# Modulation vectors moved from VectorE to TensorE, in a diffusion trunk on one Trainium2 core

## The chip, the cores and the metric

The kernel runs on one core of a Trainium2 chip. The metric is the device time of one execution in microseconds (us), taken as the median of several runs. A profile of one execution of the kernel before stands beside the runs.

## What is computed

The reference is one step of a trunk of two layers, over 512 latent tokens and 128 context tokens of 1024 features. A layer is a feed-forward half, a token mixer and a second feed-forward half. Each of the three is modulated by the condition and is followed by a layer norm:

```
def _modulation(cond, w, b):
    return (jax.nn.silu(cond) @ w + b).reshape(cond.shape[0], N_MOD, D_MODEL)

def _modulate(x, shift, scale):
    return x * (1.0 + scale[:, None, :]) + shift[:, None, :]

def _ffn_half(x, mod, slot, w1, w3, w2, g, b):
    h = _modulate(x, mod[:, 3 * slot], mod[:, 3 * slot + 1])
    f = (jax.nn.silu(h @ w1) * (h @ w3)) @ w2
    return _residual_post_norm(x, f, mod[:, 3 * slot + 2], FFN_RES, g, b)
```

There are nine modulation vectors a layer (shift, scale and gate for each of the three), for two conditions, one of the latent tokens and one of the context. `w_mod` is 1024 by 9 x 1024 for each layer, 75 MB in all. The mixer has three groups of heads: A (differential attention), B (windowed, with a sink) and C (keys and values from a compressed tensor).

## The kernel before, in words

**Layout.** Features lie on partitions in eight tiles `x[d]` of 128 by 640 tokens. Every product with a weight is done in three passes (weight hi by input hi, hi by lo, lo by hi), so each weight tile is cast on ScalarE (`wh`, L299) and the remainder taken on VectorE or GpSimd (`wl`, L306). One stream (`Stream`, L220) loads the tiles on SP's queue into two raw buffers, in the order of their products, and converts up to six blocks ahead.

**A feed-forward half** (`ffn`, L1016) goes through 22 hidden tiles in six chunks (`CHUNKS`). The first three tiles are done in the plain way; each of the other 19 is a `Pair` (L830): seven products of twelve matmuls of 320 columns, in Winograd's scheme, with the sums `pm`, `sl` and `gf` that VectorE forms from the banks (`op`, L858). `start` (L893) issues a pair's first two products, `run` (L898) the other five. What waits for a product is put in `later` and issued by `slot` (L815) after the next product. After each chunk `rows` (L631) or, in the last, `rows_norm` (L659) multiply by w2 and add to `x`. L1110 scales the gate after the first chunk, and L527 is the first product of the next norm's statistics. There are four halves, F1 to F4 in the order of the program, and a mixer after F1 and after F3.

**A modulation unit** is one vector for one feature tile, written (layer, vector, tile): 128 values for each of two conditions. There are 144. It is made in one of three ways.

1. `mod_start` (L406): sixteen passes on TensorE (`mod_mm`, L391, L397), of eight float32 matmuls with 32 weight columns each, put 128 values on four rows of a bank. VectorE copies them to `ms`. `mod_finish` (L380) puts them on partitions with a matmul with `sel` (L384) into a new bank, and VectorE adds the bias (L389). The start of the program and the first chunk of F1 use this, for 24 units.
2. `mod_beside` (L411): the same in the unused part of a bank that holds the fifth transpose of an attention unit (`Unit.t5`, L1578, and in group B where a unit has three blocks of keys). The passes go to TensorE at once; `rest` (L419), issued later, is on ScalarE: the bias for the last unit and the copy of this one. `mix_left` says how many may be started.
3. `vec_mods` (L437): VectorE multiplies rows of the transposed weights (`wmt`) by the condition that was put on all partitions (`condb`) and sums them, four instructions of 512 columns a unit (L460) and a last one (L463). `mods` (L1025), which the half calls between products, takes its next steps.

Of the 144 units, 24 go the first way, ten the second (all in mixer 0) and 110 the third: 38 in F1, 36 in F2 and 36 in F3. F4 has none.

**Loads.** `mod_load(k)` (L365) issues two loads of 256 KB for each of the next k units that aren't loaded, on SP's queue, into a pool `pm` of four buffers, two units. `mod_mm` calls it before its matmuls and after them, with the depth `mod_depth[0]`, 2. In the same queue stand the weights, the copies between partitions that the attention needs, and the transfers of `x`.

**The order in a mixer** is written out in `SCHEDULES`, one table for each layer: a letter and a number issue a stage of a unit of attention (`s` scores, `t` four transposes, `r` the fifth one with `mod_beside`, `R` its `rest`, `p` values). 40 of the 48 units of a mixer call `mod_beside`: 16 of group A, 8 of B, 16 of C.

Of the kernel before, what the change touches and what calls it, by code (L numbers as in the profile page):

```python
# [7 lines left out]
F32 = mybir.dt.float32  # L8
# [97 lines left out]
def trunk_kernel(tc, I, O):  # L106
# [3 lines left out]
    with ExitStack() as es:  # L110
# [98 lines left out]
        class W:  # L209
            """a weight tile in pieces along its contraction tiles"""  # L210
# [9 lines left out]
        class Stream:  # L220
            """jobs in the order of their products: whole tiles, or the blocks a pair of tiles is combined to"""
# [28 lines left out]
            def combine(self, r):  # L250
                """the sums of Winograd's scheme of two tiles' halves along the contraction"""
# [85 lines left out]
        def step(n=1, fill=1):  # L337
            """the oldest task's next steps, as many of the filler, and a waiting transfer"""
            for _ in range(n):
                advance(tasks)  # L340
            for _ in range(fill):
                advance(filler)
            if dmaq:
                dmaq.pop(0)()

        def start(g):
            """a task whose first step comes at once"""
            next(g)
            tasks.append(g)
# [8 lines left out]
        modq = []  # L358
        mod_queue = [nc.sync]
        mod_depth = [2]  # L360
# [30 lines left out]
        def mod_mm(ps):  # L391
# [6 lines left out]
            mod_load(mod_depth[0])  # L398
# [7 lines left out]
        def mod_start():  # L406
            """128 modulation values of the next unit, before they are put on partitions"""
            ps = bank("mod")
            mod_take(mod_mm(ps[:, :P]), ps[:, :P])

        def mod_beside(ps):  # L411
            """the same in the unused part of a bank; gives what is left to do when the bank's products are issued"""
# [16 lines left out]
        def mod_step():  # L429
            """the rest of the last unit, and the start of the next"""  # L430
            mod_finish()
            if modq:
                mod_start()

        vecq = []

        def vec_mods(n):  # L437
            """generator: the next n units on the vector engine, beside the products of a feed-forward half"""
            cb = pv.tile([P, 4, NS], F32, tag="tabs", name=f"cb{uid()}")
            nc.sync.dma_start(out=cb, in_=I["condb"])  # L440
            yield
            units, w = [vecq.pop(0) for _ in range(n)], []

            def load(k):
                while len(w) < min(k, 2 * n):
                    t = pm.tile([P, 512], F32, tag="wm", name=f"wv{uid()}")
                    hf = len(w) % 2
                    nc.sync.dma_start(out=t, in_=I["wmt"][units[len(w) // 2]][:, 512 * hf:512 * hf + 512])
                    w.append(t)
            load(4)  # L450
            for i in range(4):
                S.activation(cb[:, i, :], cb[:, i, :], AF.Silu)
                yield
            scr = u(pq, f"scr{uid()}")[:, :512]
            for i, (l, s_, d) in enumerate(units):
                a = tiny([4], "va")
                for hf in range(2):
                    load(2 * i + hf + 4)
                    for st in range(2):
                        V.scalar_tensor_tensor(out=scr, in0=w[2 * i + hf], scalar=1.0, in1=cb[:, 2 * st + hf, :], op0=ALU.mult, op1=ALU.mult,  # L460
                                               accum_out=a[:, 2 * hf + st:2 * hf + st + 1])
                        yield
                V.scalar_tensor_tensor(out=mod[l][:, s_, d, :], in0=a[:, 0:2], scalar=bmod[:, l, s_, d:d + 1], in1=a[:, 2:4], op0=ALU.add,  # L463
                                       op1=ALU.add)

# [14 lines left out]
        def mmk(out, whl, acts, half, k, ka, n):  # L480
            """the three passes of contraction tile k (of n) into a half's bank"""
# [19 lines left out]
        def acc(d, half):  # L501
            """running sums of x and x^2 over feature tiles"""
# [27 lines left out]
        def bcast(name, src, nt):  # L530
            """[P, nt] per-token values (token on its partition) to every partition, along the tokens"""
# [34 lines left out]
        def mod_hi(d, half, h):  # L566
            """hi part of x * gamma + beta"""
# [5 lines left out]
        def mod_f(d, half, kept=None):  # L573
            """x * gamma + beta, in kept when it is to stay"""
# [56 lines left out]
        def rows(acts, n, begun, each):  # L631
            """x += gate * (w^T act) for every feature tile; begun: (weights, sums, contraction tiles done) of the first ones"""
# [17 lines left out]
        def open_tiles(pn, wn, h, half, d):  # L650
            """contraction tile d of the next phase's first weight tiles, the passes that need hi first"""
# [7 lines left out]
        def rows_norm(acts, n, l, ln, nxt, begun=()):  # L659
            """the same, then the layer norm; with nxt = (layer, slot), also the next modulated input and, tile by tile  # L660
            as it comes, the first weight tiles of the next phase; begun: (weights, sums, contraction tiles done) of the
            first feature tiles"""
# [62 lines left out]
            # first half: statistics under the second half's products  # L725
# [76 lines left out]
        def alpha_x(l, ln):  # L802
            """the residual branch of what the norm left in x"""
# [9 lines left out]
        later = []  # L813

        def slot():  # L815
            """what waited for the products issued so far"""
# [13 lines left out]
        class Pair:  # L830
            """silu(w1^T h) * (w3^T h) of one hidden tile by Winograd's scheme: rows w1, w3, columns the halves of the tokens"""
# [61 lines left out]
            def start(self):  # L893
                p1, p2 = bank("p1"), bank("p2")
                self.prod(p1, self.b11, lambda: S.copy(self.m[:, LO], p1[:, :HN]) and None)
# [30 lines left out]
            def run_first(self, mods, other, ts):  # L926
                """the same with the sums of the input's quarters last, as they come, and the start of the other one before them"""
# [43 lines left out]
        def tb_steps(tb, h):  # L971
            """generator: hi and lo of the sums of the input's quarters, for the contraction tiles k and k + 4; the last ones
            take the place of the quarter that no pair reads"""
# [42 lines left out]
        def ffn(l, f, h, first, nmod, nvec, norm, scale_x, tb, ts):  # L1016
            n_left = [nmod]
            vec, credit = [None], [0.0]
            if nvec:
                cb = vec_mods(nvec)  # L1020
                next(cb)
# [3 lines left out]
            def mods(when=None):  # L1025
                if vec[0]:
                    credit[0] += (4 * nvec + 4) / 95 * (1 if when is None else 1)
                    while credit[0] >= 1:
                        credit[0] -= 1
                        next(vec[0], None)  # L1030
# [15 lines left out]
            for ci, (j0, j1) in enumerate(CHUNKS):  # L1046
                gs = []
                n = j1 - j0
                for j in range(j0, j1):
                    if j >= NC:  # L1050
# [6 lines left out]
                        if j == NC:  # L1057
                            scale_x()
                            if nvec:
                                vec[0] = cb  # L1060
# [1140 lines left out]
```

## Time and profile before

| | us |
|---|---|
| three runs | 2775.0, 2775.86, 2776.04 |
| median | 2775.86 |
| span of the profiled execution | 2768.7 |
| TensorE busy | 2541.8 (92%) |
| VectorE busy | 2257.6 (82%) |
| GpSimd busy | 1249.4 (45%) |
| ScalarE busy | 1150.4 (42%) |

The span is the time from the first to the last instruction of one profiled execution; what lies around it in a run is not in it. An engine's busy time is the time in which it executes, with waits left out. A share over the whole span mixes the halves, the mixers and the norms, whose limits differ, so the rows below are cut by stage. In them PE is TensorE, PEld its weight loads, DVE VectorE, ACT ScalarE, POOL GpSimd and SP the engine that issues the transfers.

### The profile page before, as it was taken

The numbers are of one execution on the slowest core, as the hardware profiler recorded it, in microseconds if no ns is written. First come the engines' busy times: TensorE is split into PE (matmuls) and PEld (weight loads), VectorE is DVE, ScalarE is ACT, GpSimd is POOL, SyncE is SP. The second block draws the span as 40 slices with busy tenths as digits, with TensorE's granted clock in tenths as the row PEclk, the third lists the DMA queues.
The fourth block names the chain that finished last, engine by engine and source line by source line (L and its number), as shares of the span: only waits on it lengthen the run. The fifth ranks groups of instructions, "written<-read, shape, count | busy, mean of one in ns | idle before, by whom it ended". The sixth has DMA issues, their size and how long they took to land. (4 is left out here: it accounts for less than half of the span.)

```text
span 2768.7 us, 48136 instructions
## 1 busy us (share of the span) xinstructions
PE 2541.8 (92%) x17546; PEld 2430.0 (88%) x17546; DVE 2257.6 (82%) x4315; ACT 1150.4 (42%) x2474; POOL 1249.4 (45%) x973
## 2 busy tenths in 40 slices
PE   7998899899999998888999988998898899999997
PEld 6988899888868998888889888898897689999997
DVE  6699999865875889999988999999677758777776
ACT  5232323345575533333344333333455745344333
POOL 2343453521454644434545445434333556545545
PEclk9999999999999999999989999999999999999998
DMA  7333333334212133333323333333332121222222
GB/s 265 129 120 109 115 113 125 114 118 149 74 37 92 69 115 118 122 103 112 118 69 103 116 119 113 119 126 99 120 100 60 37 99 47 82 78 89 81 85 69
DMA packets 130539, 285.77 MB, mean 103 GB/s; under 512 B 16832, under 2 KB 34560, under 8 KB 129664
## 3 DMA queue, kind: packets, MB, share of 16 engines
q1 hardware_dynamic: 130304, 282.70, 31.3%
q8 instruction: 139, 2.28, 0.3%
q14 instruction: 96, 0.79, 0.1%
HBM read 254.95 MB, written 8.81 MB: 95 GB/s over the span
## 5 line engine op out<-in xcount | busy, mean ns | idle before, releaser
L306 DVE TENSOR_TENSOR wl<-wr,wh 128x512 fp32r<-128x512 f32 (+1 forms) x524 | 499.0, 965 | 66.3 <-ACT wh L299 64.5
L299 ACT CAST wh<-wr 128x512 fp32r<-128x512 f32 (+1 forms) x570 | 331.9, 606 | 500.8 <-DMA wr<-in_w 351.8
L485 PE MATMUL o<-gh,wh 128*128 128x256 f32 (+1 forms) x1408 | 442.8, 314 | 24.8 <-ACT gh L886 13.2
L847 PE MATMUL p<-hh,wh 128*128 128x320 f32 x1216 | 387.7, 319 | 83.3 <-DVE pm L858 79.1
L485 PE MATMUL o<-gl,wh 128*128 128x256 f32 (+1 forms) x1408 | 440.7, 313 | 3.2 <-DVE gl L478 1.8
L259 POOL TENSOR_TENSOR ws<-wr 128x512 f32<-128x512 f32 x76 | 111.3, 1464 | 728.4 <-DMA wr<-in_w 548.8
L485 PE MATMUL o<-gh,wl 128*128 128x256 f32 (+1 forms) x1408 | 438.1, 311 | 0.0
L460 DVE SCALAR_TENSOR_TENSOR scr<-wv,cb 128x512 f32<-128x512 f32 x440 | 394.7, 897 | 4.2
L847 PE MATMUL p<-hl,wh 128*128 128x320 f32 x1216 | 384.7, 316 | 6.6 <-DVE hl L1010 6.6
L847 PE MATMUL p<-hh,wl 128*128 128x320 f32 x1216 | 385.5, 317 | 1.9 <-DVE wl L306 1.8
L847 PEld LDWEIGHTS p<-hh,wh 128*128 128x128 f32 x1216 | 235.6, 194 | 92.3 <-issue 78.0
L306 POOL TENSOR_TENSOR wl<-ws,wh 128x512 fp32r<-128x512 f32 x152 | 241.4, 1595 | 133.3 <-ACT wh L299 133.3
L485 PEld LDWEIGHTS o<-gh,wh 128*128 128x128 f32 x1408 | 269.3, 191 | 33.6 <-ACT gh L886 16.0
L299 ACT CAST wh<-ws 128x512 fp32r<-128x512 f32 x304 | 181.3, 619 | 247.3 <-POOL ws L259 80.6
L485 PEld LDWEIGHTS o<-gl,wh 128*128 128x128 f32 x1408 | 269.5, 191 | 8.9 <-DVE gl L891 4.9
L485 PEld LDWEIGHTS o<-gh,wl 128*128 128x128 f32 x1408 | 269.1, 191 | 0.0
L610 DVE SCALAR_TENSOR_TENSOR x<-o,gat,x 128x128 f32<-128x128 f32 (+2 forms) x404 | 192.8, 523 | 92.9 <-PE o L485 87.4
L847 PEld LDWEIGHTS p<-hl,wh 128*128 128x128 f32 x1216 | 236.1, 194 | 7.6 <-DVE hl L1010 7.6
L847 PEld LDWEIGHTS p<-hh,wl 128*128 128x128 f32 x1216 | 235.9, 194 | 4.0 <-DVE wl L306 4.0
L877 ACT ACTIVATE sl<-sl 128x320 f32<-128x320 f32 x76 | 35.8, 471 | 277.7 <-DVE sl L858 277.5
L259 POOL TENSOR_TENSOR ws<-wr,ws 128x512 f32<-128x512 f32 x76 | 130.8, 1720 | 0.0
L306 DVE TENSOR_TENSOR wl<-ws,wh 128x512 fp32r<-128x512 f32 x152 | 129.3, 863 | 0.0
(428 smaller groups left out, 6618.8 us busy)
## 6 DMA issues: line engine op xcount, KB each, us to landing
wr<-in_w SPq DMA_DIRECT2D x176, 512.0 KB, 3.8
wv<-in_wmt SPq DMA_DIRECT2D x220, 256.0 KB, 2.8
wr<-in_w SPq DMA_DIRECT2D x128, 256.0 KB, 2.6
wm<-in_wmod SPq DMA_DIRECT2D x68, 256.0 KB, 5.0
wr<-in_w SPq DMA_DIRECT2D x64, 192.0 KB, 2.4
wr<-in_wint SPq DMA_DIRECT2D x24, 512.0 KB, 3.8
wr<-in_wo SPq DMA_DIRECT2D x16, 512.0 KB, 3.8
xd<-x SPq DMA_DIRECT2D x16, 320.0 KB, 5.6
```

The costliest lines, as they stand in the source:

```text
L259: G.tensor_tensor(out=o, in0=x0, in1=x1, op=op)
L299: S.copy(hl[0], src[:, c0:c1])
L306: eng.tensor_tensor(out=t2, in0=src, in1=t.bitcast(F32), op=ALU.subtract)
L460: V.scalar_tensor_tensor(out=scr, in0=w[2 * i + hf], scalar=1.0, in1=cb[:, 2 * st + hf, :], op0=ALU.mult, op1=ALU.mult, accum_out=a[:, 2 * ...
L485: PE.matmul(out[:, :cn], whl[a][:, k, :], b[:, c0:c0 + cn], start=k == 0 and i == 0, stop=k == n - 1 and i == 2)
L610: V.scalar_tensor_tensor(out=c, in0=src, scalar=gat[:, d, s:s + 1], in1=c, op0=ALU.mult, op1=ALU.add)
L847: PE.matmul(out[:, :HN], w[a][:, k, :], b[k][c], start=k == 0 and i == 0, stop=k == 3 and i == 2)
L877: S.activation(self.sl[:, HI], self.sl[:, HI], AF.Silu)
```

## The change

No unit is made on VectorE any more. 16 units go beside a pair's first product in each of F1, F2 and F3, with the second way's code: `Pair.start` calls `mod_beside` with the 192 columns of the bank that the product leaves free, ahead of the product, and `rest` follows the copy of the product. What is pending is finished by `mod_finish` in the middle of the pair. 40 units go beside the transposes of mixer 0 and 32 beside those of mixer 1. The lists are refilled before each half and each mixer (`next_mods`). After its matmuls `mod_mm` asks for one unit ahead and no longer two.

```
-        mod_depth = [2]
+        mod_depth = [2, 2]
...
             for kk in range(2):
                 for g in range(4):
                     PE.matmul(ps[32 * g:32 * g + 32, :], silc[:, 2 * g + kk, :], w[g // 2][:, 2 * (g % 2) + kk, :], start=kk == 0, stop=kk == 1)
-            mod_load(mod_depth[0])
+            mod_load(mod_depth[1])
...
-        def vec_mods(n):
...
-                        V.scalar_tensor_tensor(out=scr, in0=w[2 * i + hf], scalar=1.0, in1=cb[:, 2 * st + hf, :], op0=ALU.mult, op1=ALU.mult,
-                                               accum_out=a[:, 2 * hf + st:2 * hf + st + 1])
-                        yield
...
             def start(self):
                 p1, p2 = bank("p1"), bank("p2")
-                self.prod(p1, self.b11, lambda: S.copy(self.m[:, LO], p1[:, :HN]) and None)
+                rest = mod_beside(p1[:, HN:])
+
+                def c1():
+                    S.copy(self.m[:, LO], p1[:, :HN])
+                    rest()
+                self.prod(p1, self.b11, c1)
                 self.prod(p2, self.b21, lambda: self.c11(p2))
...
-        def ffn(l, f, h, first, nmod, nvec, norm, scale_x, tb, ts):
+        def ffn(l, f, h, first, nmod, nside, norm, scale_x, tb, ts):
             n_left = [nmod]
-            vec, credit = [None], [0.0]
-            if nvec:
-                cb = vec_mods(nvec)
-                next(cb)
+            mix_left[0] = nside
...
-                if vec[0]:
-                    credit[0] += (4 * nvec + 4) / 95 * (1 if when is None else 1)
-                    while credit[0] >= 1:
-                        credit[0] -= 1
-                        next(vec[0], None)
...
+        def next_mods(n):
+            modq.extend(later_mods.pop(0) for _ in range(n * KD))
+
         for l in range(DEPTH):
             if l:
+                next_mods(2)
                 tb, ts = tb_next
-            h, first = ffn(l, 0, h, first, *((8, 38) if l == 0 else (0, 36)), lambda a, n, b: rows_norm(a, n, l, 0, (l, 1), b),
+            h, first = ffn(l, 0, h, first, 0 if l else KD, 2 * KD, lambda a, n, b: rows_norm(a, n, l, 0, (l, 1), b),
                            alpha_first if l == 0 else lambda: alpha_x(l - 1, 2), tb, ts)
-            if l == 0:
-                modq += [vecq.pop(0) for _ in range(10)]
+            next_mods(4 if l else 5)
             h, first = mixer(l, h, first, lambda a, n, b: rows_norm(a, n, l, 1, (l, 2), b))
             nxt = (l + 1, 0) if l + 1 < DEPTH else None
+            if l == 0:
+                next_mods(2)
             tb, ts = tb_next
-            h, first = ffn(l, 1, h, first, 0, 36 if l == 0 else 0, lambda a, n, b: rows_norm(a, n, l, 2, nxt, b),
+            h, first = ffn(l, 1, h, first, 0, 0 if l else 2 * KD, lambda a, n, b: rows_norm(a, n, l, 2, nxt, b),
                            lambda: alpha_x(l, 1), tb, ts)
```

How the order of the instructions moves is seen at three places. The first is TensorE in F1, where one pair ends (its seventh product) and the next begins; `p` is a bank, `hh` and `hl` are the parts of the input, `wh` and `wl` those of the weights. Before:

```order
L847 MATMUL p_2706<-hh_196,wh_2589 128x320
L847 MATMUL p_2706<-hl_197,wh_2589 128x320
L847 MATMUL p_2706<-hh_196,wl_2590 128x320
L847 MATMUL p_2729<-hh_182,wh_2612 128x320
L847 MATMUL p_2729<-hl_183,wh_2612 128x320
```

And with the change, at such a place, and further on the end of the pair's fourth product and the start of its fifth:

```order
L818 MATMUL p_2517<-hh_196,wh_2410 128x320
L818 MATMUL p_2517<-hl_197,wh_2410 128x320
L818 MATMUL p_2517<-hh_196,wl_2411 128x320
L397 MATMUL p_2540<-wm_2381,silc 32x128 x2
L397 MATMUL p_2540<-wm_2383,silc 32x128 x2
L397 MATMUL p_2540<-wm_2381,silc 32x128 x2
L397 MATMUL p_2540<-wm_2383,silc 32x128 x2
L818 MATMUL p_2540<-hh_182,wh_2430 128x320
...
L818 MATMUL p_2611<-hh_184,wl_2500 128x320
L384 MATMUL mod_2630<-const,ms_2589 128x2
L818 MATMUL p_2633<-tvb_693,wh_2519 128x320
```

Eight matmuls of a unit now stand ahead of the pair's first product, and the one that puts its values on partitions stands between the fourth and the fifth.

The second place is VectorE in F1 beside a pair. `scr` is the result of a unit's multiplication that nothing reads, `wl` the low part of a weight block, the others are the pair's sums. Before:

```order
L858 TENSOR_TENSOR sl_1891<-pm_1830,p_1969 128x320
L306 TENSOR_TENSOR wl_1996<-ws_1938,wh_1995 128x512
L460 SCALAR_TENSOR_TENSOR scr_1514,va_1914<-wv_1806,cb_808 128x512 x2
L881 TENSOR_TENSOR gf_1966<-gf_1966,sl_1891 128x320
L858 TENSOR_TENSOR sl_2051<-pm_1989,p_1993 128x320
L306 TENSOR_TENSOR wl_2036<-wr_1946,wh_2035 128x384
L463 SCALAR_TENSOR_TENSOR mod_144<-va_1914,const 128x2
L460 SCALAR_TENSOR_TENSOR scr_1514,va_2075<-wv_1870,cb_808 128x512 x2
L306 TENSOR_TENSOR wl_2058<-wr_1948,wh_2057 128x384
```

And with the change:

```order
L829 TENSOR_TENSOR sl_2445<-pm_2376,p_2517 128x320
L306 TENSOR_TENSOR wl_2556<-ws_2487,wh_2555 128x512
L852 TENSOR_TENSOR gf_2515<-gf_2515,sl_2445 128x320
L829 TENSOR_TENSOR sl_2609<-pm_2537,p_2541 128x320
L306 TENSOR_TENSOR wl_2594<-wr_2495,wh_2593 128x512
L389 TENSOR_SCALAR mod_144<-mod_2630,const 128x2
L306 TENSOR_TENSOR wl_2614<-wr_2495,wh_2613 128x512
```

The multiplications are gone from between the pair's sums; what is left of a unit is one instruction of two columns.

The third place is SP's queue in mixer 0, where group C's queries and keys (`C1qh` to `C1kl`) are copied to their partitions. Before:

```order
L1890 DMA C1qh_9417<-qph_8614 32x512
L1891 DMA C1kh_9419<-kph_8479 32x640
L1890 DMA C1ql_9418<-qpl_8615 32x512
L1891 DMA C1kl_9420<-kpl_8480 32x640
L1256 DMA oh_9527<-oc_9529 64x2x128 x2
```

And with the change:

```order
L374 DMA wm_9558<-in_wmod 128x512
L374 DMA wm_9560<-in_wmod 128x512
L1854 DMA C1qh_9570<-qph_8636 32x512
L1855 DMA C1kh_9572<-kph_8475 32x640
L1854 DMA C1ql_9571<-qpl_8637 32x512
L1855 DMA C1kl_9573<-kpl_8476 32x640
L374 DMA wm_9636<-in_wmod 128x512
L374 DMA wm_9638<-in_wmod 128x512
L374 DMA wm_9694<-in_wmod 128x512
L374 DMA wm_9696<-in_wmod 128x512
L1220 DMA oh_9712<-oc_9714 64x2x128 x2
```

The loads of the units (`wm`) now stand ahead of and behind those copies in one queue.

## Rows read from the trace of the kernel before

**Rows 1.** The page's head: the span, then busy time, share, instructions.

```profile
span 2768.7 us, 48136 instructions
...
PE 2541.8 (92%) x17546; PEld 2430.0 (88%) x17546; DVE 2257.6 (82%) x4315; ACT 1150.4 (42%) x2474; POOL 1249.4 (45%) x973
```

**Rows 2.** Windows: F1, F2, F3, F4 from L1110 to L527, then mixers 0 and 1.

```profile
core 0: us, PE busy (x) PEld busy (x) DVE busy (x) ACT busy (x) POOL busy (x), PEclk, DMA share, GB/s
110.70:543.00 432.30, 390.93 (x2508) 379.36 (x2507) 403.68 (x769) 139.03 (x262) 190.11 (x118) 0.97 0.36 120
992.80:1423.60 430.80, 389.25 (x2513) 380.05 (x2512) 401.05 (x751) 138.64 (x262) 191.10 (x118) 0.96 0.35 115
1508.60:1935.50 426.90, 386.34 (x2498) 376.67 (x2496) 399.46 (x751) 138.29 (x262) 191.19 (x118) 0.97 0.36 119
2373.90:2742.30 368.40, 366.67 (x2507) 366.36 (x2506) 268.32 (x422) 138.92 (x253) 179.44 (x118) 1.00 0.24 79
543.00:911.50 368.50, 341.11 (x2664) 307.77 (x2664) 247.25 (x544) 204.61 (x544) 147.48 (x157) 0.97 0.31 94
1935.50:2292.90 357.40, 331.01 (x2483) 299.75 (x2484) 248.30 (x544) 199.89 (x524) 149.66 (x157) 0.98 0.27 82
```

**Rows 3.** Windows: F2 and F4, from the second chunk's first pair on.

```profile
1016.20:1394.50 378.30, 340.80 (x2185) 332.56 (x2184) 359.88 (x673) 120.78 (x230) 167.78 (x104) 0.96 0.35 116
...
2396.40:2715.00 318.60, 318.60 (x2176) 318.60 (x2176) 239.84 (x370) 126.17 (x231) 157.12 (x103) 1.00 0.24 80
```

**Rows 4.** Waits of TensorE, whole span: us in total, times, longest us.

```profile
PE p L847 <- DVE pm L858: 79.1, 32, 4.6
```

**Rows 5.** Units' instructions on VectorE, by tile: duration ns min/median/max.

```profile
L460 DVE SCALAR_TENSOR_TENSOR scr<-wv,cb x440: 674/685/1815, 120.3 to 1914.5; 128x512 f32<-128x512 f32 x147
L460 DVE DVE_READ_ACCUMULATOR scr<-wv,cb x440: 74/79/86, 120.9 to 1915.1; 128x1 f32 x147
...
L389 DVE TENSOR_SCALAR mod<-mod,const x8: 203/208/219, 66.7 to 110.4; 128x2 f32<-128x2 f32 x8
```

**Rows 6.** Timeline of TensorE, mixer 0, a unit beside a transpose: start, duration.

```profile
639.97 0.28 PE L415 MATMUL t<-const,ms 128*128 128x2 f32 x2
640.18 0.65 PE L397 MATMUL t<-wm,silc 128*32 128x128 f32 x16
640.75 0.44 PE L485 MATMUL pj<-hh,wh 128*128 128x384 f32 x1
```

**Rows 7.** Mixer 0's units: copy, waits for loads, longest wait, KB and landing.

```profile
L425 ACT COPY ms<-t x10: 258/263/278, 637.8 to 701.5; 128x128 f32<-128x128 f32 x10
...
DMA wm<-in_wmod: 6.1, 4
...
PE t L397 <- DMA wm<-in_wmod: 2.8, 2, 2.6
...
wm<-in_wmod SPq DMA_DIRECT2D x20, 256.0 KB, 2.9
```

**Rows 8.** Windows: attention of mixers 0 and 1, then group C's transposes.

```profile
627.90:870.60 242.70, 223.43 (x1857) 193.50 (x1856) 163.67 (x394) 147.34 (x424) 97.99 (x115) 0.98 0.26 73
2017.00:2253.20 236.20, 217.94 (x1699) 190.13 (x1697) 165.03 (x397) 143.71 (x407) 99.37 (x115) 0.98 0.20 55
818.20:863.30 45.10, 39.96 (x362) 33.48 (x361) 25.37 (x75) 31.07 (x91) 18.48 (x30) 1.00 0.07 15
```

**Rows 9.** Timeline, F4, a pair's start: its next loads, first products, ScalarE's copy.

```profile
2406.62 0.80 SPq L243 DMA_DIRECT2D wr<-in_w  x2
...
2408.70 0.31 PE L847 MATMUL p<-hh,wh 128*128 128x320 f32 x1
2408.85 0.31 PE L847 MATMUL p<-hl,wh 128*128 128x320 f32 x1
...
2411.45 0.41 ACT L895 COPY pm<-p 128x320 f32<-128x320 f32 x1
```

More of the change, by code (lines that the diff above doesn't have):

```diff
@@ L433, in mod_step @@
                 mod_start()
-        vecq = []
-        def vec_mods(n):
-            cb = pv.tile([P, 4, NS], F32, tag="tabs", name=f"cb{uid()}")
-            nc.sync.dma_start(out=cb, in_=I["condb"])
-            yield
[L442 to L459, printed above, removed]
-                        V.scalar_tensor_tensor(out=scr, in0=w[2 * i + hf], scalar=1.0, in1=cb[:, 2 * st + hf, :], op0=ALU.mult, op1=ALU.mult,
-                                               accum_out=a[:, 2 * hf + st:2 * hf + st + 1])
-                        yield
-                V.scalar_tensor_tensor(out=mod[l][:, s_, d, :], in0=a[:, 0:2], scalar=bmod[:, l, s_, d:d + 1], in1=a[:, 2:4], op0=ALU.add,
-                                       op1=ALU.add)
+        later_mods = []
         ev = [0]
@@ L1058, in ffn @@
                             scale_x()
-                            if nvec:
-                                vec[0] = cb
                         continue
@@ L1115, in ffn @@
                     step(0, 1)
-                    for _ in vec[0] or ():
-                        pass
                     if f == 0:
@@ L2054, in mods_of @@
                 nc.sync.dma_start(out=x[d + 1], in_=I["xT"][d + 1])
-            mod_depth[0] = 6
+            mod_depth[:] = 6, 6
         def into_h(d):
@@ L2080, in trunk_kernel @@
                 modq += [(0, 2, d) for d in range(KD)]
-                vecq += [(0, s, d) for s in range(3, 9) for d in range(KD)]
-                vecq += [(1, s, d) for s in range(9) for d in range(KD)]
-                mod_depth[0] = 2
+                later_mods += [(0, s, d) for s in range(3, 9) for d in range(KD)]
+                later_mods += [(1, s, d) for s in range(9) for d in range(KD)]
+                modq += [later_mods.pop(0) for _ in range(2 * KD)]
+                mod_depth[:] = 2, 1
                 mod_pool[0] = pm
@@ L2139 @@
     arr["wmod"] = X["w_mod"].reshape(L, KD, P, 9, KD, P).transpose(0, 3, 4, 2, 1, 5)
-    arr["wmt"] = X["w_mod"].reshape(L, D, 9, KD, P).transpose(0, 2, 3, 4, 1)
-    arr["condb"] = np.broadcast_to(np.stack([X["c"][0], X["c_ctx"]]).reshape(1, 4, 512), (P, 4, 512))
     small["bmod"] = X["b_mod"].reshape(L, 9, KD, P).transpose(3, 0, 1, 2)
```

## The prediction

> **What bounds the kernel now.** I read the page first: the span is 2768.7 us, TensorE is busy for 92% of it and VectorE for 82% [rows 1]. A kernel with TensorE at 92% looks as if VectorE could be unloaded for nothing, so the next view has to go by stage. The three sets of windows cut each feed-forward half from the instruction that scales its gate (L1110) to the first product of the statistics (L527), and each mixer from one such product to the next [rows 2]. Call the halves F1 to F4 in their order. F1, F2 and F3 each take over 425 us and carry 38, 36 and 36 units of modulation on VectorE. F4 has the same products and no units: it takes 368.40 us. The number of matmuls is the same within ten (2508, 2513, 2498 and 2507). The difference is therefore no work of TensorE: F1 to F3 hold VectorE for about 400 us and grant TensorE a mean clock of 0.96 to 0.97 of its 2.4 GHz, with stretches at 1.2, F4 holds VectorE for 268 us and grants 1.00 [rows 2]. The inner stretch, all but the first of the halves' pairs and rows, says it sharper: 378.30 us with TensorE busy for 340.80 in F2, and 318.60 us with TensorE busy for 318.60 in F4 [rows 3]. The list of waits names what TensorE waits for: the sum `pm` that VectorE reads out of a bank, 79.1 us [rows 4]. So F1 to F3 are bound by VectorE, which empties the banks late because it stands between units, and F4 is bound by TensorE alone. F4 is a run of the changed half without its new matmuls, in the same execution. The mixers are mixed: TensorE is busy for 341.11 of 368.50 and 331.01 of 357.40 us, the first with ten units beside its transposes and the second with none [rows 2].
>
> **The change, part by part.** (1) Removed from F1 to F3: 440 products of a weight row with the condition, median 0.685 us and 0.079 us for the read of the accumulator [rows 5], with a last sum for each of the 110 units. These are some 336 us of VectorE before any slowing. I don't price them by that, since TensorE feels only the part that makes banks late. The price is F4's: 432.30 + 430.80 + 426.90 less three times 368.40 is **184.8 us taken off** [rows 2]. The loads go too, two of 256 KB for a unit, and as many come back for the same unit on TensorE, so the traffic stays.
>
> (2) Added in F1 to F3: 16 units each, 48 in all, ahead of a pair's first product in the same bank. One unit is 16 passes and, later, two passes that put it on partitions. In mixer 0 the two passes begin at 639.97, the sixteen at 640.18 and the next product at 640.75 [rows 6]: 0.78 us of TensorE a unit. In F4 nothing hides it, so 48 x 0.78 = **37.4 us**. The trace has no such unit between two products of a pair. Below, the bound is the 0.57 us of the sixteen passes alone (27.4 us); above, the 0.78 with one product's whole modelled duration of 0.31 us [rows 9] for each of two changes of shape, 1.40 us (67 us). I take 0.78, the row of the thing itself, with other products before and behind it.
> The Trainium skill, "TensorEngine Tiling (Array Packing)", section Tiling Modes, says that tiles of a 128x32 shape run in parallel but that changing the mode drains TensorE, which speaks against putting such a unit in the middle of a full run. By parallel running alone, an estimate from its four tiles and from rows 9 (0.15 us for 320 columns, so 0.06 for 128, four at once) would give the sixteen passes 0.24 us in place of 0.57 and the sum 36 us less over 110 units. The row's 0.57 lies between that and 0.96 for sixteen one after the other; the trace decides, and it has the changes of mode in it.
>
> (3) What a unit costs elsewhere in a pair. ScalarE copies the 128 values: 0.263 us [rows 7]. In F4 the copy of the pair's first product starts at 2411.45 for a pair that begins at 2408.70 [rows 9], so the values are there some 3.5 us after the pair's start, and the two passes come after four products of twelve matmuls at 0.15 us, at 7 us: no wait. VectorE adds the bias, 0.208 us [rows 5], behind work that F4 shows it has time for. Nothing is charged.
>
> (4) The loads. In a half, SP issues the next unit's two loads when the present pair begins, after the pair of weight tiles, which F4 issues at 2406.62 for a pair at 2408.70 [rows 9]; the next pair starts 84 matmuls, some 12.5 us, later, and such a load lands in 2.9 us [rows 7]. That is covered. The units of F2 and F3 and those of mixer 1 start from an empty list, so the first one's load is issued where it is used; mixer 0 shows that wait, 2.6 us of the 2.8 in the list [rows 7]. Three such waits, each from 0 to two landings, 5.8 us; I take 3 each: **9 us**.
>
> (5) Added in the mixers: 62 units, 30 and 32 more than now. By TensorE's passes they cost 62 x 0.78 = 48.4 us. The two mixers of the trace bound this: with ten units against none, the whole mixer is 11.1 us longer [rows 2], 1.11 a unit with its waits, and the stretch of the attention from the first fifth transpose to the return of x is 242.70 against 236.20 us [rows 8], 6.5, or 0.39 a unit when the first wait of 2.6 is taken out. The ends are 24 and 69 us. I take the middle, which is also the passes' own time: **48.4 us**.
>
> (6) The queue of SP in group C of the mixers. The units' loads now stand between the copies for group C's keys and queries, which wait for ScalarE, VectorE or GpSimd, and are issued one unit ahead where they were issued two ahead. In the present trace the units of group A waited 6.1 us in four waits for their loads with ten units [rows 7]; without the first, 0.35 us a unit. Group C's fifth transposes come every 3 us (45.10 us for 15 intervals [rows 8]), or 3.8 with a unit, and a load lands in 2.9. It has room while SP is free. For the 24 units there (16 and 8) I take 0.35 each, **8.4 us**, between nothing and a whole landing each, 70 us.
>
> The sum is -184.8 + 37.4 + 9 + 48.4 + 8.4 = **-81.6 us** against the profiled execution, whose span of 2768.7 us stands 7.2 us under the median of the runs, 2775.86. Start and end lie outside the change, so the 7.2 stays: 2775.86 - 81.6 is about **2694 us**.
>
> **The rivals.** (a) The mixers hide more. Their TensorE is idle for 27.4 and 26.4 us [rows 2], and a unit beside a transpose that waits for GpSimd's scaling costs nothing. At 0.39 a unit they cost 24.2 us in place of 48.4, and with no wait in group C the 8.4 go: 2694 - 32.6 is about 2661 us. For it speaks the attention's stretch, against it that the whole mixer shows 1.11.
> (b) Group C becomes bound by the units' loads and ScalarE's small copies. ScalarE is busy for 31.07 of 45.10 us there [rows 8], and the copy of the fifth block waits for the unit's passes, being in one bank with them. At 1.11 a unit and half a landing, 1.45 us, for each of the 24 units, the mixers cost 68.8 + 34.8 in place of 56.8: 2741 us. For it speaks that the loads are one unit ahead only; against it, that two intervals of 3.8 us stand against a landing of 2.9.
> (c) **Slower than before.** One mechanism: in the mixers the loads stand behind SP's other copies, TensorE meets each unit before its weights, and stops for a whole landing. At 62 x 2.9 = 180 us in place of the 8.4 the time is 2694 + 171 = 2865 us. The point from which it decides is a mean wait of (184.8 - 37.4 - 9 - 48.4) / 62 = 1.45 us a unit, four times the 0.35 that rows 7 give. Against it: ten units in the busiest part of SP's queue, with 16 small copies for each group of keys, waited 3.5 us in all after the first.
> (d) The halves don't reach F4's pace. If the units break the run enough to keep the clock at F1's 0.97 instead of 1.00, 3% of three halves, 33 us, come back: 2727 us. Against it: a unit is 0.57 us of products with no pause.
> (e) F4 is fast for another reason, and the change frees VectorE without doing for the halves what F4 shows. Then half of the 184.8 would be left: 2786 us. Against it: the same number of matmuls, and the waits named in rows 4 are for VectorE. I give it 0.02.
>
> **How the numbers follow.** The forecast has 0.58, (a) 0.17, (b) 0.12, (c) 0.03, (d) 0.08, (e) 0.02. A difference of 0.2%, 5.6 us, is about what a measurement of this kernel can tell from no change. Faster by more than that are the forecast, (a), (b) and (d), 0.95; within it some of what lies between (b) and (e), 0.02; slower (c) and part of (e), 0.03. The range goes from 2655, a little under (a), to 2728, with (d). It leaves out (b), (c) and (e), 0.17 together, and takes in the bounds of parts 2, 4 and 5 taken singly (2694 - 24 and 2694 + 30 at the most).
>
> **What would show it.** In the profile after, F1 to F3 between the same instructions take 368 + 12 = 380 us each, at a clock of 1.00, with TensorE busy all through and no wait for `pm`; VectorE's busy time falls by the 400 us that F1 to F3 have over F4, to about 1860. The mixers take about 397 and 388 us. Waits of TensorE for `wm` stay under 30 us in all. I am wrong in part 1 if F1 to F3 stay above 400 us, in part 5 or 6 if a mixer grows by more than 45 us, and in the whole if waits for `wm` exceed 90 us.

## The result and the profile after

The changed kernel takes 2709.78 us, the median of four runs (2709.09 to 2714.02), against 2775.95 for the kernel before beside it (four runs, 2775.0 to 2777.23). The ratio is 0.976, with a 95% interval of 0.9737 to 0.9783. That is faster, inside the range, and 16 us above the number.

The page of the kernel after, first the span, then the engines' busy times:

```profile
span 2707.7 us, 51139 instructions
...
PE 2583.2 (95%) x19526; PEld 2471.6 (91%) x19526; DVE 1870.3 (69%) x3374; ACT 1185.8 (44%) x2633; POOL 1201.4 (44%) x973
```

VectorE lost 387.3 us of work, TensorE gained 41.4 and the span lost 61.0 [rows 1]. The windows tell where, cut as in [rows 2] and with the same columns. The first six are F1, F2, F3, F4 and mixers 0 and 1:

```profile
112.40:497.49 385.09, 381.94 (x2779) 375.30 (x2777) 273.06 (x442) 143.35 (x272) 177.41 (x118) 1.00 0.33 102
983.75:1369.45 385.70, 383.19 (x2780) 376.65 (x2779) 273.99 (x442) 143.45 (x272) 176.30 (x118) 1.00 0.32 99
1458.25:1843.69 385.44, 383.01 (x2780) 376.34 (x2779) 275.92 (x442) 143.46 (x272) 177.53 (x118) 1.00 0.32 102
2311.38:2680.66 369.28, 367.54 (x2512) 367.24 (x2512) 265.26 (x422) 138.68 (x253) 178.34 (x118) 1.00 0.25 79
497.49:897.78 400.29, 370.34 (x3203) 333.37 (x3204) 248.81 (x546) 214.11 (x602) 148.28 (x157) 0.96 0.42 126
1843.69:2229.53 385.84, 358.77 (x3060) 322.14 (x3060) 243.96 (x544) 210.77 (x588) 147.74 (x157) 0.98 0.40 120
...
897.78:983.75 85.97, 77.34 (x515) 74.82 (x515) 67.71 (x116) 42.42 (x84) 49.44 (x45) 0.96 0.20 61
1369.45:1458.25 88.80, 77.13 (x491) 74.55 (x491) 69.26 (x119) 43.61 (x86) 49.84 (x45) 0.90 0.20 60
```

F1 to F3 are now 47.2, 45.1 and 41.5 us shorter than in [rows 2], at a granted clock of 1.00, with TensorE idle for 2 to 3 us. The mixers are 31.8 and 28.4 us longer. The last two rows are the stretches ahead of F2 and F3, from the end of the window before: 85.97 and 88.80 us, where the bounds of [rows 2] leave 81.30 and 85.00, so 4.7 and 3.8 more. The start, F4, the stretch ahead of it and the end make up the other 4 us.

The span fell by 61.0 us and the median by 66.2. The profiled execution of the kernel before stood 7.2 us under its median, that of the kernel after 2.1 under its own, so 5 us of the difference are in which execution was profiled, and no stage accounts for them.

The waits of TensorE for the units' weights, over the whole span (columns as in [rows 4]); the wait for `pm` that [rows 4] show is gone:

```profile
PE p L397 <- DMA wm<-in_wmod: 14.2, 2, 7.2
PE t L397 <- DMA wm<-in_wmod: 12.0, 12, 2.9
...
PE tr L397 <- DMA wm<-in_wmod: 1.3, 4, 0.5
```

Last, TensorE's timeline in the kernel after, at three places: a unit ahead of a pair's first product in F1, the first unit of F2, and the two passes that end a unit in F2 (start, duration, line, output and operands):

```profile
161.49 0.31 PE L818 MATMUL p<-hh,wl 128*128 128x320 f32 x1
161.72 0.64 PE L397 MATMUL p<-wm,silc 128*32 128x128 f32 x16
162.30 0.41 PE L818 MATMUL p<-hh,wh 128*128 128x320 f32 x1
162.55 0.31 PE L818 MATMUL p<-hl,wh 128*128 128x320 f32 x1
162.70 0.31 PE L818 MATMUL p<-hh,wl 128*128 128x320 f32 x1
...
955.54 0.34 PE L456 MATMUL h<-hh,wl 128*128 128x384 f32 x1
962.80 1.77 PE L397 MATMUL p<-wm,silc 128*32 128x128 f32 x16 [6.92 <-DMA wm<-in_wmod]
964.50 0.64 PE L818 MATMUL p<-hh,wh 128*128 128x320 f32 x1
...
1014.40 0.31 PE L818 MATMUL p<-hh,wl 128*128 128x320 f32 x1
1014.54 0.28 PE L384 MATMUL mod<-const,ms 128*128 128x2 f32 x2
1014.68 0.39 PE L818 MATMUL p<-tvb,wh 128*128 128x320 f32 x1
1014.91 0.31 PE L818 MATMUL p<-tr,wh 128*128 128x320 f32 x1
```

Durations overlap, so read the starts. A plain product starts 0.15 us after the one ahead of it (162.55 to 162.70). At 161.49 the next one but one starts at 162.55, 1.06 us later in place of 0.29: 0.77 us for the sixteen passes. Of these 0.58 are the passes themselves; the product ahead of them takes 0.23 and the one behind 0.25 where a plain one takes 0.15. At 1014.40 it is 0.51 in place of 0.29: 0.22 us for the two passes, of which the product behind them has 0.08. A unit in a half costs **0.99 us**.

### The profile page after: what moved, and what is told of

The parts are those of the page before. It is cut to its first block, busy times and chain, and to the rows that moved or that the text cites. A ratio compares the mean times of both kernels' runs of the same rounds, so it can differ in the third digit from the quotient of the medians.

```text
span 2707.7 us, 51139 instructions
## 1 busy us (share of the span) xinstructions
PE 2583.2 (95%) x19526; PEld 2471.6 (91%) x19526; DVE 1870.3 (69%) x3374; ACT 1185.8 (44%) x2633; POOL 1201.4 (44%) x973
## 5 line engine op out<-in xcount | busy, mean ns | idle before, releaser
L306 DVE TENSOR_TENSOR wl<-wr,wh 128x512 fp32r<-128x512 f32 (+1 forms) x524 | 505.7, 977 | 60.4 <-ACT wh L299 58.6
L299 ACT CAST wh<-ws 128x512 fp32r<-128x512 f32 x304 | 188.2, 621 | 462.2 <-PE p L818 290.8
L818 PE MATMUL p<-hl,wh 128*128 128x320 f32 x1216 | 377.3, 310 | 2.0 <-DVE hl L986 2.0
L818 PE MATMUL p<-hh,wl 128*128 128x320 f32 x1216 | 377.2, 310 | 0.0
L306 POOL TENSOR_TENSOR wl<-ws,wh 128x512 fp32r<-128x512 f32 x152 | 224.7, 1478 | 330.1 <-ACT wh L299 325.5
L818 PEld LDWEIGHTS p<-hl,wh 128*128 128x128 f32 x1216 | 229.7, 189 | 2.2 <-DVE hl L986 2.2
L818 PEld LDWEIGHTS p<-hh,wl 128*128 128x128 f32 x1216 | 229.7, 189 | 0.0
L259 POOL TENSOR_TENSOR ws<-ws,wr 128x512 f32<-128x512 f32 x76 | 117.9, 1551 | 6.0
L259 POOL TENSOR_TENSOR ws<-wr,wr 128x512 f32<-128x512 f32 x76 | 118.2, 1556 | 0.0
L818 PE MATMUL p<-tq,wh 128*128 128x320 f32 x456 | 116.7, 310 | 0.0
```

What stands on the lines that cost most here:

```text
L259: G.tensor_tensor(out=o, in0=x0, in1=x1, op=op)
L299: S.copy(hl[0], src[:, c0:c1])
L306: eng.tensor_tensor(out=t2, in0=src, in1=t.bitcast(F32), op=ALU.subtract)
L818: PE.matmul(out[:, :HN], w[a][:, k, :], b[k][c], start=k == 0 and i == 0, stop=k == 3 and i == 2)
```

## The experiments

Expectations and results are given in the order of the runs. The first two edit the kernel before, the others the changed one.

**VectorE's units taken out** (kernel before). Does F4's pace hold for the other halves?

```
-*((8, 38) if l == 0 else (0, 36))
+*((8, 0) if l == 0 else (0, 0))
...
-0, 36 if l == 0 else 0,
+0, 0,
```

> The kernel before, with the 110 units of F1, F2 and F3 left out and put nowhere (their modulation values stay at zero). Theory of the prediction (VectorE, standing between units, empties the banks late): F1 to F3, which took 432, 431 and 427 us, come to F4's 368 to 371 us, and the time falls by 180 to 190 us against before. Rival (e), F4 is fast for a reason of its own: F1 to F3 stay above 400 us and the time falls by under 95 us.

Measured: 2589.93 us, ratio 0.9335 [0.9308, 0.9362] to the kernel before, some 184 us less. The windows, F1 to F3:

```profile
110.07:480.19 370.12, 367.99 (x2507) 367.34 (x2506) 271.55 (x426) 140.93 (x258) 180.02 (x118) 1.00 0.26 86
930.80:1301.75 370.95, 367.80 (x2513) 367.31 (x2512) 273.37 (x427) 140.90 (x257) 179.88 (x118) 1.00 0.26 83
1382.91:1753.13 370.22, 368.04 (x2509) 367.19 (x2507) 276.24 (x427) 141.00 (x257) 179.70 (x118) 1.00 0.27 86
```

The halves without units run at F4's pace within 3 us and at its clock.

**The same units without their loads** (kernel before). The units are still multiplied on VectorE, from weights that lie in the chip already.

```
-t = pm.tile([P, 512], F32, tag="wm", name=f"wv{uid()}")
-hf = len(w) % 2
-nc.sync.dma_start(out=t, in_=I["wmt"][units[len(w) // 2]][:, 512 * hf:512 * hf + 512])
+t = cb[:, len(w) % 4, :]
```

> The kernel before, with the units' instructions left on VectorE but without the 220 loads of their weights: they multiply the condition by itself, so the values are not the modulation. Theory (VectorE's time): F1 to F3 stay between 422 and 432 us and the time within 8 us of before. Rival (the loads in SP's queue, or their traffic, held the halves): F1 to F3 fall under 400 us and the time by more than 80 us.

Measured: 2773.63 us, ratio 0.9992 [0.9981, 1.0004]. F2 in the windows:

```profile
993.10:1424.10 431.00, 389.25 (x2513) 380.57 (x2512) 407.41 (x751) 139.03 (x262) 187.65 (x118) 0.96 0.22 72
```

The DMA share falls from 0.35 to 0.22 [rows 2] and the time does not move. What held F1 to F3 was VectorE's time, not its loads; with the run before, rival (e) falls.

**The halves' units left out** of the changed kernel, those of the mixers kept:

```
-modq += [later_mods.pop(0) for _ in range(2 * KD)]
+del later_mods[:2 * KD]
...
-next_mods(2)
+del later_mods[:2 * KD]
...
```

The number of units that a half may start is set to 0 as well.

> The changed kernel, with the 48 units of the halves left out (their values stay at zero); the mixers' 72 are as they were. Theory (a unit in a half costs 0.99 us of TensorE, 0.77 for the sixteen passes with the slower matmuls at their two ends and 0.22 for the two passes, and the first one of F2 and F3 stops for its load): F1 to F3 go from 385 us to 369 to 371, the stretches ahead of F2 and F3 from 86 and 89 us to 81 to 85, and the time falls by 50 to 60 us. Rival (0.78 us a unit as predicted, and the other 4 us a half come from VectorE's or ScalarE's part of the new order): F1 to F3 stay at 373 us or more and the time falls by under 45 us.

Measured: 2650.1 us, 0.9552 [0.9524, 0.958]. F1 and F2:

```profile
111.21:481.84 370.63, 368.26 (x2508) 368.06 (x2507) 269.03 (x427) 140.96 (x258) 179.00 (x118) 1.00 0.27 85
958.30:1329.17 370.87, 367.67 (x2513) 367.17 (x2511) 272.67 (x427) 141.00 (x257) 178.55 (x118) 1.00 0.26 83
```

F3 takes 370.51 us. The units cost 14.5, 14.8 and 14.9 us a half (385.09, 385.70 and 385.44 above). In each half the first pair, and with it the first of the 16 units, lies ahead of the window; 15 times 0.99 is 14.9. The timeline's price holds for the stage, and the time falls by 59.7 us, as the theory said.

**The mixers' units left out**, those of the halves kept:

```
-next_mods(4 if l else 5)
+del later_mods[:(4 if l else 5) * KD]
```

> The changed kernel, with the 72 units of the mixers left out (their values stay at zero); the halves' 48 are as they were. Theory (about 0.97 us a unit, passes and a few waits): the mixers go from 400 and 386 us to 357 to 364 and 352 to 358, and the time falls by 65 to 78 us. Rival (a), the mixers hide most of a unit: the time falls by under 45 us. Rival (b), group C stands behind the loads: over 90 us.

Measured: 2640.25 us, 0.9517 [0.9489, 0.9544]. Mixers 0 and 1:

```profile
498.68:858.88 360.20, 329.08 (x2484) 298.03 (x2485) 247.39 (x544) 201.85 (x524) 148.32 (x157) 0.98 0.29 82
1806.80:2165.45 358.65, 333.08 (x2483) 301.44 (x2484) 247.68 (x544) 200.28 (x524) 147.71 (x157) 0.97 0.28 82
```

So 40 units cost mixer 0 40.1 us, and 32 cost mixer 1 27.2; the time falls by 69.5 us, as the theory said. In mixer 0 TensorE's busy time grew by 41.3 (370.34 - 329.08), at a granted clock of 0.96 in place of 0.98: its idle time, 31 us without units and 30 with them, was not used at all.

**One list** for all units, so that no half or mixer begins with an empty one:

```
-modq += [later_mods.pop(0) for _ in range(2 * KD)]
+modq += later_mods
...
-mix_left[0] = len(modq)
+mix_left[0] = 32 if l else 40
...
```

The calls of `next_mods` are left out.

> The changed kernel, with all units in one list from the start, so that the load of the first unit of F2, F3 and each mixer is issued when the last unit of the stage before is done, long ahead; nothing else. Theory (the stops of 7 us at the first pair of F2 and F3 are pure waits for a load that is issued where it is used): the stretches ahead of F2 and F3 go from 86 and 89 us to 82 and 85, the mixers lose 1 to 3 us each, and the time falls by 8 to 20 us. Rival (behind those stops another wait ends no earlier, a weight block or a bank): the time stays within 3 us.

Measured: 2688.7 us, 0.9676 [0.9658, 0.9693], against the change's 0.976. The stretches ahead of F2 and F3, and TensorE's waits in the first of them:

```profile
891.82:973.56 81.74, 77.27 (x519) 74.94 (x519) 69.14 (x116) 42.33 (x84) 51.18 (x45) 0.98 0.19 58
1358.50:1443.45 84.95, 77.88 (x502) 74.89 (x503) 70.44 (x120) 43.41 (x86) 51.95 (x45) 0.94 0.18 57
```

```profile
PE p L818 <- DVE hl L986: 2.0, 1, 2.0
...
PE p L818 <- DVE tm L986: 0.9, 1, 0.9
```

Both stretches get shorter, by 4.2 and 3.9 us. That is less than the stops of 7 us. Ahead of F2 the reason is that two waits for VectorE, 2.9 us, appear again, which the change does not have there: while TensorE waited for the load, VectorE caught up. Ahead of F3 another wait stands instead, for ScalarE's copy of a unit:

```profile
PE mod L384 <- ACT ms L425: 2.8, 1, 2.8
```

Mixer 0 gains 7.6 us, part of it in the norm at its start, which takes between 37.6 and 41.1 us in one execution or another, whatever the kernel: 40.90 us at a granted clock of 0.87 in the change, 38.90 at 0.91 here. Mixer 1 is 0.8 us longer, where the theory had 1 to 3 us less.

**The two passes beside the unit.** On top of the last edit, the pending unit is finished with the next unit instead of in the middle of the pair:

```
-mod_finish()
+if when is None:
+    mod_finish()
```

> As e5, and a unit's two passes stand ahead of the next unit's sixteen in the next pair's bank, with the bias on ScalarE, in place of between the fourth and fifth product. Theory (what a unit costs over its bare passes lies at the places where TensorE changes between its products and a unit, one fewer here): F1 to F3 take 1 to 2 us less each than in e5 and the time 2 to 6 us less. Rival (the places don't matter, only the passes): within 1.5 us of e5.

Measured: 2686.66 us, 0.9667 [0.965, 0.9684]. F1 and F2 fell by 0.9 and 0.8 us and F3 rose by 0.7, where a fall of 1 to 2 was expected of each. The medians are 2 us apart, well inside the intervals: inconclusive.

**Two units ahead**, as in the kernel before:

```
-mod_depth[:] = 2, 1
+mod_depth[:] = 2, 2
```

> The changed kernel, with two units asked for after a unit's matmuls, as before, in place of one. Theory (asking for the second one makes SP wait in its queue until the present unit's matmuls are done, and everything behind waits too): the mixers take 2 to 10 us more together, the halves stay, the time rises by 2 to 10 us. Rival (the earlier request spares TensorE the 13 us in which it waits for loads in the mixers): the time falls by 4 to 10 us.

Measured: 2687.48 us, 0.9671 [0.9653, 0.9688], 22 us under the change. The mixers, then TensorE's wait for weights beside the transposes:

```profile
496.80:882.65 385.85, 360.51 (x3205) 325.19 (x3205) 247.48 (x545) 213.51 (x602) 147.82 (x157) 0.98 0.43 131
1826.64:2206.29 379.65, 354.78 (x3060) 320.06 (x3060) 247.03 (x544) 210.50 (x588) 148.63 (x157) 0.98 0.41 122
```

```profile
PE t L397 <- DMA wm<-in_wmod: 3.9, 4, 2.2
...
SPq L374 <- PE t L397: 110.6, 38, 9.0
SPq L374 <- PE p L397: 74.8, 41, 4.9
SPq L374 <- PE tr L397: 39.8, 12, 5.6
```

My theory lost to its rival, and the gain is over twice the 4 to 10 us of the rival. The theory was that a second unit ahead holds SP in its queue until a buffer comes free, and so delays the copies behind it. It does hold SP longer, 110.6, 74.8 and 39.8 us in the rows above (SP's waits; in the change these are 69.7, 6.8 and 11.9), and TensorE's one wait for another transfer in the mixers (`rp`) stays as it was, 3.1 us in the change and 2.8 here. The mixers are 14.4 and 6.2 us shorter (3.2 of the first is the norm at the start). TensorE's waits for `wm` beside transposes fell by 9.4 us (12.0 + 1.3 to 3.9), but more of the gain, 13.8 us, is TensorE's busy time: 9.8 us less in mixer 0, where the granted clock rises from 0.96 to 0.98 (the 3.2 us of the norm are in this: it ran at 0.95 here and at 0.87 in the change), and 4.0 in mixer 1.

With the loads in time, the units' own price can be read against the bare mixers: TensorE is busy for 31.4 us more in mixer 0 and 21.7 in mixer 1, **0.79 and 0.68 us a unit**, and is idle for 5.8 and 0.7 us less. Mixer 0 has a clock of 0.98 in both runs. Mixer 1 has 0.97 bare and 0.98 here; an estimate of what that hides is 1% of 333 us, 0.1 us a unit, so at an equal clock its price is near 0.78 too.

**Full width.** In the halves a unit's passes use all 128 columns, as the products do, instead of four tiles of 32, so that the shape does not change:

```
+for k in range(KD if wide else 0):
+    PE.matmul(ps, silc[:, 2 * k:2 * k + P], w[k // 4][:, k % 4, :], start=k == 0, stop=k == KD - 1)
...
-rest = mod_beside(p1[:, HN:])
+rest = mod_beside(p1[:, HN:], True)
```

> The changed kernel, with the units of the halves made by eight matmuls of all 128 weight columns into one bank, one after the other, in place of four times 32 columns side by side. Theory (the slower matmuls at the two ends of a unit, 0.09 and 0.10 us, come from changing the shape of the array): they vanish, the sixteen passes take 16 times 0.06 us, about 0.9 to 1.0, in place of 0.57 and a unit 0.1 to 0.25 us more than now; F1 to F3 take 2 to 4 us more each. Rival (the slower ends belong to float32 matmuls of any shape): a unit takes 0.3 to 0.5 us more and F1 to F3 5 to 8 us more each.

Measured: 2753.0 us, 0.9909 [0.989, 0.9928], 43 us over the change. A pair's start in F1:

```profile
151.09 0.31 PE L820 MATMUL p<-hh,wl 128*128 128x320 f32 x1
151.24 1.95 PE L396 MATMUL p<-wm,silc 128*128 128x128 f32 x16
152.94 0.39 PE L820 MATMUL p<-hh,wh 128*128 128x320 f32 x1
153.17 0.31 PE L820 MATMUL p<-hl,wh 128*128 128x320 f32 x1
```

Both expectations were too low: F1 and F2 take 15.8 and 15.0 us more. Sixteen passes take 1.70 us, 0.11 each, and not the 0.06 that I had worked out from the products' columns. But the row separates the prices. The passes now begin 0.15 us behind the product, like a product, so the extra 0.08 ahead of the narrow ones goes with the change of shape. Leaving the shape has a price too, inside the 0.58 us of the narrow passes. These are the last pass of the unit in the change and the last one at full width:

```profile
162.10 0.27 PE L397 MATMUL p<-wm,silc 128*32 128x128 f32 x1
...
152.91 0.28 PE L396 MATMUL p<-wm,silc 128*128 128x128 f32 x1
```

The next product starts 0.20 us behind the narrow one (162.30) and 0.03 behind the wide one (152.94), 0.17 less. So of a unit's 0.99 us some 0.25 go with the two changes of shape. The product behind the passes still takes 0.23, so most of the extra in that one does not.

The Trainium skill, "TensorEngine Tiling (Array Packing)", section Tiling Modes, says that tiles work in parallel and that a change of mode drains TensorE. The first shows here: sixteen narrow passes take 0.58 us where sixteen full ones take 1.70. The 0.08 us on the way in and the 0.17 on the way out agree with the second; the traces show these delays and not a drain itself.

**The three edits together** (one list, passes beside the unit, two units ahead).

> The changed kernel with the edits of e5, e6 and e7 together: one list, a unit's end in the next pair's bank, two units asked for ahead. Theory (e5 and e6 repair the first pairs of F2 and F3, the depth of two repairs the mixers, and the two hardly overlap): the stretches ahead of F2 and F3 at 82 to 85 us, the mixers at 378 to 386 and 374 to 381, the time 8 to 18 us under that of e7. Rival (e5 and e7 save the same waits): within 5 us of e7.

Measured: 2673.5 us, 0.9628 [0.9606, 0.9649], 14 us under the run with two units ahead. The stretches ahead of F2 and F3 take 81.77 and 85.44 us. Mixers 0 and 1:

```profile
497.25:885.97 388.72, 364.45 (x3205) 328.79 (x3205) 248.99 (x546) 214.26 (x602) 147.81 (x157) 0.97 0.43 130
1819.39:2195.72 376.33, 352.91 (x3061) 317.79 (x3060) 246.05 (x543) 210.21 (x588) 149.12 (x157) 0.99 0.40 120
```

This version beats both kernels: 36 us under the change, run again beside it. TensorE's list of waits has no row for `wm` left in a half or a mixer. Mixer 0 is longer than expected; its norm at the start took 41.1 us here, 3.4 more than in the run with two units ahead.

**One load for a whole mixer.** The first unit's weights serve all units of the mixer:

```
 for unit in modq[:k]:
+    if fixed and fixed[0]:
+        modw[unit] = fixed[0]
     if unit not in modw:
...
         modw[unit] = w
+        if fixed:
+            fixed[0] = w
...
```

> The changed kernel, depth one as it is, but in each mixer the weights of the first unit are loaded once and used for all its units (the values of the others are wrong); all passes stay. Theory (the mixers' extra over the passes is the wait for loads that are asked for one unit ahead): the mixers go from 400 and 386 us to 374 to 385 and 372 to 380, the time falls by 18 to 35 us. Rival (the loads cost little, and a unit's passes and copies take their 1 us): the mixers stay above 393 and 383 us and the time falls by under 10 us.

Measured: 2688.99 us, 0.9681 [0.9659, 0.9702], 20.8 us under the change; the mixers take 388.40 and 382.53 us, above what I had expected of them, with 4.9 us of waits beside the transposes left. Passes without loads are no faster than passes with loads asked for two units ahead (385.85 and 379.65). The loads' traffic is gone here and nothing more is gained, so what the mixers pay above the passes is the late request.

**The change once more**, beside these two:

> The changed kernel as it is, to stand beside e9 and e10 on one chip: a ratio to before of 0.974 to 0.978.

Measured: 2709.8 us, 0.9753 [0.9729, 0.9776]; the mixers took 399.46 and 388.93 us. Here mixer 0's norm took 37.6 us, as in the run with two units ahead, so these mixers against that run's give the late request without the norm: 13.6 + 9.3 = 22.9 us.

## Why the prediction held, and where its terms were off

The sum was -81.6 us; the span moved by -61.0. Of the 20.6 us between them 13.6 are in the halves' windows, 2.5 in the stretches ahead of F2 and F3 (8.5 for the 6 of two waits), 0.4 in the mixers, and 4 in the start, F4, the stretch ahead of it and the end, for which I had nothing. Term by term:

**Part 1 (-184.8), right.** The halves without units take 370.1 to 371.0 us where F4 said 368.4: 6 us less in all than I took. An undisturbed stage of the same execution priced the removal of 336 us of VectorE's work to within 6 of 185 us, and the run without loads shows that the work was the cause.

**Part 2 (+37.4), too small.** The step that failed is "I take 0.78, the row of the thing itself": a unit in a half costs 0.99, 47.5 us for 48. In [rows 6] I had counted from the start of the two passes to the start of the next product. The neighbours are slower as well: the product ahead of the sixteen passes takes 0.23 us, the one behind them 0.25 and the one behind the two passes 0.23, each instead of 0.15, 0.26 more in all. The two passes themselves take 0.14 here, 0.07 less than in the row. The halves' windows came 13.6 us above the forecast: 6 from part 1, and 7.5 from this, since three of the 48 units lie ahead of them.

**Part 3 (nothing), right.** No wait for a unit's copy or its bias stands in the list of TensorE's waits of F1, F2 or F3; in F2 it is busy for 383.19 of 385.70 us.

**Part 4 (+9), right in size by luck.** I had three waits of 3 us. There were two stops of 7 us, ahead of F2 and F3, and 1.7 us at mixer 1's first unit. I had taken the load to be issued when TensorE needs it; SP's rows ahead of F2 show it issued 2.9 us after the last product began, four loads at once, behind the next pair's weight tiles (`wr`), for which SP had waited 17.2 us until VectorE was done with `wl`. TensorE goes on 4.4 us later:

```profile
957.49 0.88 SPq L243 DMA_DIRECT2D wr<-in_w  x2
958.42 1.85 SPq L374 DMA_DIRECT2D wm<-in_wmod  x4
```

Each stop costs its stretch 4 us, as the run with one list shows; ahead of F2 it hides 2.9 us of waits for VectorE that the stretch has without it. It also costs what I had not counted: the passes behind it take 1.70 us instead of 0.58 (962.80 to 964.50), at a granted clock of 0.50 and with 0.5 us of waiting for the unit's second load.

**Parts 5 and 6 (+56.8), the sum right by luck, its split wrong.** With one wait of part 4 the forecast for the mixers was 59.8 us, and they grew by 60.2. But with two units ahead the 62 more units cost 17.35 + 22.25 = 39.6 us, or 43 with an equal norm: 0.64 to 0.69 each against 0.78, a step towards the 0.39 of rival (a). The 0.78 was right for TensorE's own work at an equal clock; the idle time that the units use makes the rest. And the request one unit ahead, which I priced at 8.4, costs 20.6 to 22.9. The step that failed is "For the 24 units there": the late request is paid for in both mixers, most of it in group A (whose own waits in [rows 7] had given the 0.35), and not as TensorE's waits alone. From the first product behind its norm to the first of group B's scores mixer 0 takes 6.7 us more in the change than with two units ahead, at a lower clock (the change, then the run with two units ahead):

```profile
538.39:694.59 156.20, 145.63 (x1180) 138.33 (x1179) 93.11 (x190) 76.23 (x213) 40.00 (x29) 0.93 0.48 137
...
534.50:684.00 149.50, 142.02 (x1180) 134.70 (x1179) 92.82 (x190) 76.04 (x213) 39.48 (x29) 0.97 0.50 147
```

In mixer 1 the same stretch takes 149.40 and 144.90 us. Rival (b) spoke from the same cause, loads one unit ahead only, but put it in group C, where it had 34.8 us; group C of mixer 0 takes 74.0 us in the change and 71.0 with two units ahead.

**The rivals.** (c) did not come: waits for `wm` are 27.5 us in all behind the start of the program, 13.3 of them in the mixers, 0.21 us for each of the 62 units, a seventh of the 1.45 from which it decides. (d) did not either: the clock in F1 to F3 is 1.00. (e) fell with the run without VectorE's units, where F1 to F3 come to F4's pace.

**What would show it.** VectorE's busy time, the waits under 30 us, the vanished wait for `pm` and the mixers (400.3 and 385.8 against 397 and 388) came as said; the halves took 385, not 380.

## What to carry to other kernels

Price a removal by a stage of the same execution that already runs without the work, and not by the busy time of the engine that loses it. Price an added matmul from the start of the matmul ahead of it to the start of the second one behind it, since the neighbours are slower too. Where work moves onto the engine that sets the time, ask for its loads two uses ahead and never let the list run empty between stages: either was worth some 20 us here, and both together, with the passes beside the unit, 36 of 2710.

## What the runs showed of the hardware

A stop slows what comes behind it. The windows of the kernel after, around the first unit of F2: the stop, the 5 us behind it, and the 15 behind those:

```profile
955.80:962.80 7.00, 0.08 (x2) 0.03 (x1) 6.08 (x10) 3.20 (x7) 3.34 (x2) 0.87 0.59 169
962.80:967.80 5.00, 4.93 (x28) 4.05 (x29) 2.03 (x5) 0.00 (x0) 0.00 (x0) 0.50 0.21 79
967.80:983.00 15.20, 15.20 (x107) 15.20 (x106) 8.63 (x17) 6.41 (x13) 9.45 (x9) 1.00 0.26 71
```

After 7 us in which TensorE did nothing, the granted clock is 0.50, the lower level of 1.2 GHz, for 5 us of full work, and 1.00 (2.4 GHz) behind them: 28 matmuls start in these 5 us and 107 in the 15.20 that follow. A shorter stop can do it too: the first unit of mixer 0 waits 2.9 and 0.9 us for its two loads, up to 586.5, and the granted clock from 585.6 to 595.7 is 0.50.

Sixteen float32 passes of 128 columns take 1.70 us at full width and 0.58 as four tiles of 32 side by side; entering the narrow shape costs 0.08 us, and leaving it 0.17 of the 0.58. The product behind a unit's passes takes 0.10 us more than a plain one; 0.08 of this remains at full width, where no shape changes, and what causes it was not tried.
